# Splitting the second mixer's input and the first mixer's attention rows into high and low parts, and starting the last accumulators from transposes

## The chip, the cores and the metric

The kernel runs on one core of a Trainium2 chip. The metric is the device time of one execution in microseconds; several runs are taken and their median is compared. One further execution is recorded by the profiler, and all profile rows come from that one.

The engines that matter here: PE multiplies matrices, DVE (VectorE) and ACT (ScalarE) do the elementwise work, and SP issues the DMAs that bring weights from HBM into SBUF. Each engine runs its own queue in order and waits on the others where it needs their results.

## The reference

It is a two-layer decoder trunk in float32 for one sequence of 256 positions and 1024 channels:

```python
def mixer_ab(h, w_in, conv_w, ln_g, ln_b, w_out):      # layer 0
    u = h @ w_in
    u_val, u_gate, q, k, v = jnp.split(u, ...)
    ya = conformer_conv(u_val, u_gate, conv_w, ln_g, ln_b)
    yb = moba_attention(q, k, v)
    return jnp.concatenate([ya, yb], axis=-1) @ w_out

def mixer_c(h, w_in, conv_w, conv_b, w_r, b_r, w_i, b_i, lam, w_out):   # layer 1
    u = h @ w_in
    gate, xr = jnp.split(u, 2, axis=-1)
    xr = causal_depthwise_conv(xr, conv_w) + conv_b
    y = rg_lru(xr, w_r, b_r, w_i, b_i, lam) * jax.nn.gelu(gate)
    return y @ w_out

def sq_relu_mlp(h, w_up, w_down):
    return jnp.square(jax.nn.relu(h @ w_up)) @ w_down

def reference(x, ...):
    for layer in range(2):
        x = x + mixer(rmsnorm(x, mix_norm[layer]), ...)
        x = x + sq_relu_mlp(rmsnorm(x, mlp_norm[layer]), w_up[layer], w_down[layer])
    return rmsnorm(x, final_norm)
```

`rg_lru` applies block-diagonal gate matrices (8 blocks of 128 x 128 for r and for i) and a scan over the positions. `w_up` is 1024 x 4096, `w_down` 4096 x 1024. All weights, some 97 MB, are read once.

## The kernel before

**Layout.** The residual stream lives in SBUF transposed: eight tiles `xT[k]`, 128 channels by 256 positions. A product is 128 rows of a weight by 128 columns (the stationary operand) times a 128 x 256 activation tile, summed over k in a PSUM bank. There are four banks `bank_a` (accumulators of output projections) and four banks `bank_b` (everything else).

**Weights.** They come in pieces of 1 MB, two DMAs of 512 KB each; a piece has two units, and a unit is 128 x 1024 weights, eight products. A piece lands either in one of five `raw` buffers or in one of eight pairs `wh`/`wl`, used as plain storage. `piece` decides this with a counter: after five unsplit pieces in a row the next ones go to pairs.

**Two kinds of product.** An unsplit unit is multiplied in plain fp32: one instruction per product, which the profile shows as two records. A split unit lies in a raw buffer first; `weights` rounds it to `wh` (two moves of 128 x 512, on ACT or DVE, line 395 or 396) and subtracts to get `wl` (two DVE subtractions of 128 x 512). The activation is split likewise by `split_act`, and the product is three matmuls in fp32r: high by high, high weight by low activation, low weight by high activation. In the kernel before, only the MLP weights are split. Both mixers' weights are unsplit.

**Order of the work.** Nothing is issued when the Python code runs. The calls (`mms`, `tt`, `move`, `act`, `dma`, ...) add operations to a `Plan`, with an estimated cost on each engine; the plan then schedules all of them as a list, chooses ACT or DVE for each `move`, and emits them (line 310, so that almost every row of the profile names line 310). The order on each engine is therefore fixed before the run, and a change in one place can move instructions on every engine.

**Stages in the profile.** First mixer to about 125 us: projections, attention, a layer norm whose sums over channels are made by matmuls with `ones`, and the output projection over eight units `u_o` (4 to 7 are the attention rows, 0 to 3 the convolution rows). First MLP to about 308 us: 32 units of `w_up` and 32 of `w_down`, interleaved. Second mixer to about 398 us: eight units `u_xr` (recurrent branch: `xr_proj`, `xr_tail` with the convolution of width 4, `gates`, the scan) and eight units `u_gt` (`gate_chunk`), then the output projection `u_co`. Second MLP to the end. `residual_chunk` adds an output projection to `xT` and makes the next stage's activations; `finish_norm` makes 1/rms (`rstd`), which is multiplied in later, after the first products.

**The last residual.** In the second MLP the down projection is computed the other way round: the activation is the stationary operand, and five accumulators (`blocks`) hold positions by channels, so that the output needs no transposing. `xT` must be transposed into them to be added. `down_rows` does it at the steps 4 to 19: it splits `xT[k]` into high and low (tiles `r`), and multiplies each with an identity `identr`, 32 matmuls in all.

Of the kernel before, what the change touches and what calls it, by code (L numbers as in the profile page):

```python
# [7 lines left out]
F32R = mybir.dt.float32r  # L8
# [3 lines left out]
P = 128  # L12
S = 256
# [313 lines left out]
def hybrid_trunk(ctx, tc, x, mix_norm, mlp_norm, w_up, w_down, ab_w_in, ab_conv_w, ab_ln_g, ab_ln_b,  # L327
# [8 lines left out]
    def tl(name, shape=(P, S), dt=F32):  # L336
        return sb.tile(list(shape), dt, name=name)
# [48 lines left out]
    def copy(out, a):  # L386
        return plan.add("V", [("tensor_copy", (out, a), {})], [out], [a], {"V": vcost(fsize(out), not is_psum(a))})
# [37 lines left out]
    def transposes(items):  # L425
        calls = [("transpose", (o, i, d), {}) for o, i, d in items]
        return plan.add("T", calls, [items[0][0]], [i for _, i, _ in items] + [items[0][2]],
                        {"T": 0.109 * len(items)})

    def dma(out, in_, size):  # L430
        return plan.add("S", [("dma_start", (out, in_), {})], [out], [in_], {"S": 0.0}, size=size)


    ident = tl("ident", (P, P))
    identr = tl("identr", (P, P), F32R)
    ones = tl("ones", (P, P))
    pcol = tl("pcol", (P, P))
    wcol = tl("wcol", (P, P))
# [60 lines left out]

    pieces, units = [], []
    homes, pairs = [], {}
    turn = {"raw": 0, "pair": 0, "whole": 0}

    def piece(kind, ap, whole=True):
        n = len(pieces)
        pieces.append((kind, ap))
        us = [len(units), len(units) + 1]  # L510
        units.extend([(n, 0), (n, 1)])
        turn["whole"] = turn["whole"] + 1 if whole else 0
        if turn["whole"] > NRAW:
            i = turn["pair"] % NSPL
            turn["pair"] += 1
            homes.append((whs[i], wls[i]))
        else:
            raw = raws[turn["raw"] % NRAW]
            turn["raw"] += 1
            homes.append((raw[:, :1024], raw[:, 1024:]))  # L520
        if not whole:
            for u in us:
                pairs[u] = turn["pair"] % NSPL
                turn["pair"] += 1
        return us

    def cols(w, c, whole=True):

        return piece("c", w.rearrange("(k p) c -> p k c", p=P)[:, :, c * P:(c + 2) * P], whole)

    def rows(ap, whole=True):
        return piece("r", ap, whole)

    taken = [0, 0]
    got = {}
# [51 lines left out]
    for us in (((u_gate, 4), (u_val, 0)), ((u_q, 8), (u_k, 12))):  # L587
        for c in (0, 2):
            for u, at in us:
                u += cols(w_in, at + c)  # L590
    u_v = rows(wv[:, 0:4]) + rows(wv[:, 4:8])
    wo = ab_w_out[0].rearrange("(k p) c -> p k c", p=P)
    u_o = {}
    for k in (4, 6, 0, 2):
        u_o[k], u_o[k + 1] = rows(wo[:, k:k + 2])
    LAG, TAIL = 4, 4

    def mlp_units(layer):
        up, dn = [], []
        wd = w_down[layer].rearrange("(f p) c -> p f c", p=P)  # L600
        for f in range(0, NF + LAG, 2):
            if f < NF:
                up += cols(w_up[layer], f, False)
            if f >= LAG:
                dn += rows(wd[:, f - LAG:f - LAG + 2], False)
        return up, dn

    u_up, u_dn, u_xr, u_gt, u_co = {}, {}, [], [], []
    u_up[0], u_dn[0] = mlp_units(0)
    for c in range(0, 8, 2):  # L610
        u_xr += cols(c_w_in[0], 8 + c)
        if c == 2:
            u_r, u_i = piece("ri", None)
    for c in range(0, 8, 2):
        u_gt += cols(c_w_in[0], c)
    wco = c_w_out[0].rearrange("(k p) c -> p k c", p=P)
    for k in range(0, 8, 2):
        u_co += rows(wco[:, k:k + 2])
    u_up[1], u_dn[1] = mlp_units(1)


# [9 lines left out]
    xsrc = x[0].rearrange("(t p) d -> p t d", p=P)  # L631
    R = lambda ap: ap.rearrange("a (b p) -> (a b) p", p=P)
    make_identity(nc, ident)
    copy(identr, ident)
    memset(ones, 1.0, "V")
    memset(eps_t, EPS, "V")
    act(tiny[:, 60:61], eps_t, AF.Sqrt)
# [29 lines left out]
    def par(name, c):  # L667
        i = col0[name] + c
        return pcol[:, i:i + 1]


    def project(dst, u, xs):
        w = weights(u)
        for k in range(KD):
            mms([(dst, w[k], xs[k], k == 0, k == KD - 1)])

    def project_wide(b, u, xs):

# [19 lines left out]

    def residual_chunk(k, acc, gname, g0, xs):
        tt(xT[k], acc, xT[k], OP.add)  # L700
        g = par(gname, g0 + k)
        xs[k] = scaled(xT[k], g) if gname == "mix" else split_act(xT[k], g, "x", KD)
        if k in (0, KD - 2):
            act(ssum if k == 0 else sumb, xT[k], AF.Square)
        else:
            sq = rot("nsq", 2)
            act(sq, xT[k], AF.Square)
            if k < KD - 2:
                tt(ssum, ssum, sq, OP.add)
            else:  # L710
                tt(sumb, sumb, sq, OP.add)
# [136 lines left out]
    def pv(h):  # L848
        c, r = divmod(h, 2)
        if r == 0:  # L850
            oB[c] = bank("b")
        vs = slice(64 * h, 64 * h + 64)
        up, lo = (oB[c][:, u * P + 64 * r:u * P + 64 * r + 64] for u in range(2))
        mms([(up, pT[h][:, P:S], vt[:, 0, vs], r == 0, False), (up, pT[h][:, S:384], vt[:, 1, vs], False, True)])
        mms([(lo, pT[h][:, :P], vt[:, 0, vs], False, True)])
        if r == 0:
            return
        den, o = dens[c], arot("of", 2, S)
        recip(den, den)
        n = list(den.ap)  # L860
        wide = bass.AP(tensor=den.tensor, offset=den.offset, ap=[n[0], [1, 4], [0, 64]])
        tt(o.rearrange("p (a b) -> p a b", a=4), oB[c][:, :S].rearrange("p (a b) -> p a b", a=4), wide, OP.mult)
        b = bank("b")
        transposes([(b[:, u * P:(u + 1) * P], o[:, (1 - u) * P:(2 - u) * P], ident) for u in range(2)])
        mx[4 + c] = arot("mo", 4, S)
        move(mx[4 + c], b[:, :S])

    for c in range(2, 4):
        gate_unit(c)
# [61 lines left out]
        t = [bank("a") for _ in range(4)]  # L931
        return [t[c // 2][:, (c % 2) * S:(c % 2 + 1) * S] for c in range(KD)]

    def out_mm(acc, c, w, xp, start, stop):
        if not isinstance(w, tuple):
            return mms([(acc, w[c], xp, start, stop)])
        mms([(acc, a[:, c, :], b, start and n == 0, stop and n == 2)
             for n, (a, b) in enumerate(((w[0], xp[0]), (w[0], xp[1]), (w[1], xp[0])))])

    def out_rows(accs, u, xp, first):  # L940
        w = weights(u)
        for c in range(KD):
            out_mm(accs[c], c, w, xp, first and c % 2 == 0, False)

    def out_cols(accs, us, xps, done):
        ws = [weights(u) for u in us]
        for c0 in range(0, KD, 2):
            for c in (c0, c0 + 1):
                for i, (w, xp) in enumerate(zip(ws, xps)):
                    out_mm(accs[c], c, w, xp, False, i == len(us) - 1)  # L950
            done(c0)
            done(c0 + 1)

# [52 lines left out]
    out_cols(accs, us, hs, next_norm(accs, "mix", KD, xs))  # L1006


    for t in ("lg", "pT", "of", "mo"):
        pools.pop(t)  # L1010
    top[0] = 0
    spx = ar(3, KD)
# [128 lines left out]

    blocks = []

    def down_mm(block, w, hp, first, last):
        t, c0, c1, b = block
        s = slice(t * P, (t + 1) * P)
        wh, wl = (q.rearrange("p a b -> p (a b)")[:, c0:c1] for q in w)
        mms([(b[:, :c1 - c0], p[:, s], q, first and n == 0, last and n == 2)
             for n, (p, q) in enumerate(((hp[0], wh), (hp[1], wh), (hp[0], wl)))])

    xsp = {}

    def down_rows(u, hp, d):
        w = weights(u)
        if d == 0:
            blocks.extend((t, c0, c1, bank("a")) for t, c0, c1 in ((0, 0, 512), (0, 512, D), (1, 0, 512), (1, 512, 768)))
            blocks.append((1, 768, D, banks["b"].pop(bank_at["b"] % 4)))
        for block in blocks:
            down_mm(block, w, hp, d == 0, False)
        if 4 <= d < 20:  # L1160

            k, t = divmod(d - 4, 2)
            if t == 0:
                xsp[k] = split_act(xT[k], None, "r", 2)
            for bt, c0, c1, b in blocks:
                if bt == t and c0 <= k * P < c1:
                    mms([(b[:, k * P - c0:(k + 1) * P - c0], q[:, t * P:(t + 1) * P], identr, False, False)
                         for q in xsp[k][:2]])

    _, us, hs = mlp(1, xs, down_rows)  # L1170
    ws = [weights(u) for u in us]
# [2 lines left out]
    for n, block in enumerate(blocks):  # L1174
        t, c0, c1, b = block
        xg, fc = xg2[t], fcol[:, t]
        for i in range(len(us)):
            down_mm(block, ws[i], hs[i], False, i == len(us) - 1)

        part = fc[:, n % 2 if n < 2 else n - 2:][:, :1]  # L1180
        act(fsq[:, :c1 - c0], b[:, :c1 - c0], AF.Square, accum=part)
        tt(xg[:, c0:c1], b[:, :c1 - c0], gfin[:, c0:c1], OP.mult)
        if c1 < D:
            ts(fc[:, 4:5], part, 1.0 / D, EPS if c0 == 0 else fc[:, 4:5], OP.mult, OP.add)
            continue
        act(fc[:, 5:6], part, AF.Sqrt, scale=1.0 / D, bias=fc[:, 4:5])
        recip(fc[:, 6:7], fc[:, 5:6])
        for h in (slice(0, 512), slice(512, D)):
            move(xg[:, h], xg[:, h], fc[:, 6:7])
            dma(o_dst[:, t, h], xg[:, h], P * 2048)  # L1190
# [32 lines left out]
```

## Time and profile before

| | us |
|---|---|
| median of 3 runs | 589.08 (588.99 to 589.18) |
| the profiled execution | 588.62 |
| its span, first to last instruction | 586.8 |
| PE busy | 579.9 (99%) |
| DVE busy | 413.1 (70%) |
| ACT busy | 289.7 (49%) |

A group row reads: line, engine, operation, output <- inputs with shapes, count | busy time in all, mean ns of one | idle time of the engine just before, and which engine's work ended that idle time. A timeline row reads: start, length in us, engine, line, operation, count. Rows of the chain that ended last read: start, length, engine and tile, count. Buffer numbers are left out of names in the profile. Because instructions of one engine overlap at their ends, the distance from one start to the next is shorter than the duration.

### The profile page before, as it was taken

The numbers are of one execution on the slowest core, as the hardware profiler recorded it, in microseconds if no ns is written. First come the engines' busy times: TensorE is split into PE (matmuls) and PEld (weight loads), VectorE is DVE, ScalarE is ACT, GpSimd is POOL, SyncE is SP. The second block draws the span as 40 slices with busy tenths as digits, with TensorE's granted clock in tenths as the row PEclk, the third lists the DMA queues.
The fourth block names the chain that finished last, engine by engine and source line by source line (L and its number), as shares of the span: only waits on it lengthen the run. The fifth ranks groups of instructions, "written<-read, shape, count | busy, mean of one in ns | idle before, by whom it ended". The sixth has DMA issues, their size and how long they took to land.

```text
span 586.8 us, 9026 instructions
## 1 busy us (share of the span) xinstructions
PE 579.9 (99%) x3305; PEld 510.2 (87%) x3305; DVE 413.1 (70%) x946; ACT 289.7 (49%) x592; POOL 2.8 (0%) x22
## 2 busy tenths in 40 slices
PE   9999999999999999999999999999999999999995
PEld 8888768889999999999998888888888888888885
DVE  2599998599777767677446777559876767767732
ACT  4131435467554555555321798327555555545523
POOL 1000000000000000000000000000000000000000
PEclk9999999999999999999999999999999999999999
DMA  7997704125664665566677005924645664563001
GB/s 222 324 382 256 258 1 144 71 70 163 203 212 145 191 217 166 166 205 203 218 223 280 1 0 157 370 83 143 196 164 180 196 198 144 185 212 107 1 1 72
DMA packets 67612, 98.74 MB, mean 168 GB/s; under 512 B 3212, under 2 KB 55664, under 8 KB 67568
## 3 DMA queue, kind: packets, MB, share of 16 engines
q1 hardware_dynamic: 67568, 98.17, 50.7%
q8 instruction: 26, 0.43, 0.3%
q14 instruction: 18, 0.15, 0.1%
HBM read 97.11 MB, written 1.05 MB: 167 GB/s over the span
## 4 chain that ended last, share of the span: by engine, by line
PE 99%; ACT 0%; DVE 0%; issue 0%; ACTq 0%
PE bank_b L310 56%; PE bank_a L310 42%; ACT arena L395 0%; DVE arena L310 0%; ACT arena L310 0%; DVE ones L310 0%; DVE tiny L310 0%; DVE eps L310 0%; ACTq L310 0%
## 5 line engine op out<-in xcount | busy, mean ns | idle before, releaser
L310 DVE TENSOR_TENSOR wl<-raw,wh 128x512 fp32r<-128x512 f32 x256 | 175.1, 690 | 84.5 <-ACT wh L395 76.3
L395 ACT ACTIVATE wh<-raw 128x512 fp32r<-128x512 f32 x223 | 139.5, 630 | 168.2 <-PE bank_b L310 104.3
L310 PE MATMUL bank_b<-x,wh 128*128 128x512 f32 x512 | 184.7, 401 | 0.0
L310 PE MATMUL bank_b<-x,wl 128*128 128x256 f32 x512 | 143.8, 281 | 0.0
L310 PEld LDWEIGHTS bank_b<-x,wh 128*128 128x128 f32 x512 | 96.4, 188 | 20.9
L310 PEld LDWEIGHTS bank_b<-x,wl 128*128 128x128 f32 x512 | 96.8, 189 | 0.1
L310 PE MATMUL bank_a<-f,wh 128*128 128x256 f32 x512 | 93.2, 283 | 0.0
L310 PEld LDWEIGHTS bank_a<-f,wh 128*128 128x128 f32 x512 | 79.6, 191 | 1.4
L310 PE MATMUL bank_a<-f,wl 128*128 128x256 f32 x256 | 72.4, 283 | 0.0
L310 PE MATMUL bank_a<-wh,f 128*128 128x512 f32 (+1 forms) x256 | 72.2, 364 | 0.0
L310 PE MATMUL bank_b<-xg,raw 128*128 128x256 f32 x288 | 64.1, 379 | 0.0
L310 PEld LDWEIGHTS bank_b<-xg,raw 128*128 128x128 f32 x288 | 54.1, 190 | 7.3
L310 PEld LDWEIGHTS bank_a<-wh,f 128*128 128x128 f32 x256 | 45.9, 188 | 9.1
L310 DVE SCALAR_TENSOR_TENSOR arena<-arena,wcol 128x256 f32<-128x256 f32 x120 | 49.5, 478 | 0.0
L310 PEld LDWEIGHTS bank_a<-f,wl 128*128 128x128 f32 x256 | 49.0, 192 | 0.0
L310 PE MATMUL bank_a<-wl,f 128*128 128x512 f32 (+1 forms) x128 | 46.5, 363 | 0.0
L310 PE MATMUL bank_a<-arena,wh 128*128 128x256 f32 x128 | 34.4, 381 | 0.0
L310 PE MATMUL bank_a<-arena,wl 128*128 128x256 f32 x128 | 33.9, 379 | 0.0
L310 DVE TENSOR_TENSOR relu<-bank_b,relu 128x256 f32<-128x256 f32 x64 | 26.7, 417 | 10.1 <-ACT relu L310 10.1
L310 ACT ACT_TABLE_LOAD x24 | 30.8, 1283 | 3.0 <-PE bank_b L310 1.9
L310 ACT ACTIVATE relu<-relu 128x256 f32<-128x256 f32 x64 | 26.1, 411 | 8.2 <-DVE relu L310 5.1
L310 ACT ACTIVATE relu<-bank_b 128x256 f32<-128x256 f32 x64 | 23.6, 369 | 11.6 <-PE bank_b L310 11.6
(125 smaller groups left out, 594.3 us busy)
## 6 DMA issues: line engine op xcount, KB each, us to landing
raw<-in_w_up_dram SPq DMA_DIRECT2D x64, 512.0 KB, 5.7
raw<-in_w_down_dram SPq DMA_DIRECT2D x64, 512.0 KB, 4.8
raw<-in_c_w_in_dram SPq DMA_DIRECT2D x8, 512.0 KB, 5.4
raw<-in_ab_w_in_dram SPq DMA_DIRECT2D x6, 512.0 KB, 7.8
wh<-in_ab_w_in_dram SPq DMA_DIRECT2D x5, 512.0 KB, 8.7
wl<-in_ab_w_in_dram SPq DMA_DIRECT2D x5, 512.0 KB, 8.8
raw<-in_ab_w_in_dram SPq DMA_DIRECT2D x8, 256.0 KB, 5.7
wh<-in_ab_w_out_dram SPq DMA_DIRECT2D x4, 512.0 KB, 10.0
```

Of the source, the lines that this page charges most:

```text
L310: r.append(getattr(self.engines[o.eng], method)(*map(sub, a), **{n: sub(v) for n, v in k.items()}))
L395: return e.activation(sub(out), sub(a), AF.Copy, **({"scale": scale} if ap else {}))
```

## The change

It has four parts.

1. The input weights of the second mixer (`u_xr`, `u_gt`, 16 units) become split units, and their activations come from `split_act`. `project` uses a new function `mm`, which does one plain product for an unsplit unit and three fp32r matmuls for a split one.
2. The attention rows of the first output projection (`u_o[4]` to `u_o[7]`) become split units; the attention outputs `mx[4..7]` are split straight from the PSUM bank, in place of a move.
3. The place of each piece is named at its call ("raw", "pair" or "split") in place of the counter. With it, the r and i gate weights and `c_w_out` go to pairs.
4. The last residual: 16 transposes (fp32 through `ident`) of `xT` start the five accumulators at step 0. The splits of `xT`, the 32 matmuls with `identr`, and `identr` itself go.

```diff
+    def flip(out, in_, first):
+        return plan.add("T", [("matmul", (out,), {"lhsT": in_, "rhs": ident, "start": first, "stop": False, "is_transpose": True,
+                                                  "skip_group_check": True})], [out], [in_, ident], {"T": 0.109})
...
-    identr = tl("identr", (P, P), F32R)
...
-    def piece(kind, ap, whole=True):
+    def piece(kind, ap, place):
...
-        turn["whole"] = turn["whole"] + 1 if whole else 0
-        if turn["whole"] > NRAW:
+        if place == "pair":
             i = turn["pair"] % NSPL
...
-        if not whole:
+        if place == "split":
             for u in us:
                 pairs[u] = turn["pair"] % NSPL
...
-                u += cols(w_in, at + c)
-    u_v = rows(wv[:, 0:4]) + rows(wv[:, 4:8])
+                u += cols(w_in, at + c, "raw" if len(pieces) < NRAW else "pair")
+    u_v = rows(wv[:, 0:4], "pair") + rows(wv[:, 4:8], "pair")
...
-        u_o[k], u_o[k + 1] = rows(wo[:, k:k + 2])
+        u_o[k], u_o[k + 1] = rows(wo[:, k:k + 2], "split" if k > 3 else "pair")
...
-        u_xr += cols(c_w_in[0], 8 + c)
+        u_xr += cols(c_w_in[0], 8 + c, "split")
         if c == 2:
-            u_r, u_i = piece("ri", None)
+            u_r, u_i = piece("ri", None, "pair")
...
-        u_gt += cols(c_w_in[0], c)
+        u_gt += cols(c_w_in[0], c, "split")
...
-        u_co += rows(wco[:, k:k + 2])
+        u_co += rows(wco[:, k:k + 2], "pair")
...
+    def mm(dst, w, k, x, first, last):
+        ps = ((w[0][:, k], x[0]), (w[0][:, k], x[1]), (w[1][:, k], x[0])) if isinstance(w, tuple) else ((w[k], x),)
+        mms([(dst, a, b, first and n == 0, last and n == len(ps) - 1) for n, (a, b) in enumerate(ps)])
...
-            mms([(dst, w[k], xs[k], k == 0, k == KD - 1)])
+            mm(dst, w, k, xs[k], k == 0, k == KD - 1)
...
-        xs[k] = scaled(xT[k], g) if gname == "mix" else split_act(xT[k], g, "x", KD)
+        xs[k] = split_act(xT[k], par(gname, g0 + k), "x", KD)
...
-        mx[4 + c] = arot("mo", 4, S)
-        move(mx[4 + c], b[:, :S])
+        mx[4 + c] = split_act(b[:, :S], None, "x", KD)
...
         if d == 0:
...
+            for t, c0, c1, b in blocks:
+                for k in range(c0 // P, c1 // P):
+                    flip(b[:, k * P - c0:(k + 1) * P - c0], xT[k][:, t * P:(t + 1) * P], k * P == c0)
         for block in blocks:
-            down_mm(block, w, hp, d == 0, False)
-        if 4 <= d < 20:
-            k, t = divmod(d - 4, 2)
-            if t == 0:
-                xsp[k] = split_act(xT[k], None, "r", 2)
-            for bt, c0, c1, b in blocks:
-                if bt == t and c0 <= k * P < c1:
-                    mms([(b[:, k * P - c0:(k + 1) * P - c0], q[:, t * P:(t + 1) * P], identr, False, False)
-                         for q in xsp[k][:2]])
+            down_mm(block, w, hp)
```

**Where instructions moved.** Rows are in the order in which an engine runs them; a name's numbers are those of buffers and of their uses.

DVE in the second mixer, from the reciprocal of the norm on, before:

```order
L310 RECIPROCAL rstd<-rstd 128x256
L310 TENSOR_TENSOR arena<-bank_b_108,rstd 128x256
L310 TENSOR_TENSOR arena<-bank_b_109,rstd 128x256
L310 TENSOR_SCALAR arena<-arena,pcol 128x256 x2
L310 SCALAR_TENSOR_TENSOR arena<-arena,pcol 128x256 x6
L310 TENSOR_TENSOR arena<-bank_b_111,rstd 128x256
```

and now:

```order
L310 RECIPROCAL rstd<-rstd 128x256
L396 CAST wh_1_443<-raw_71 128x512
L310 TENSOR_TENSOR arena<-bank_b_107,rstd 128x256
L310 TENSOR_TENSOR arena<-bank_b_108,rstd 128x256
L310 TENSOR_SCALAR arena<-arena,pcol 128x256 x2
L310 SCALAR_TENSOR_TENSOR arena<-arena,pcol 128x256 x2
L310 TENSOR_TENSOR wl_1_700<-raw_71,wh_1_443 128x512
L310 SCALAR_TENSOR_TENSOR arena<-arena,pcol 128x256 x3
L310 TENSOR_TENSOR wl_1_700<-raw_71,wh_1_443 128x512
L310 SCALAR_TENSOR_TENSOR arena<-arena,pcol 128x256
L310 TENSOR_TENSOR arena<-bank_b_110,rstd 128x256
```

The convolution steps of `xr_tail` (the rows with `pcol`) now have the weights' subtractions (`wl`) among them.

PE at the second MLP's first down rows; before, one of the residual's pairs of products, and now the transposes, ahead of the first product into the accumulators:

```order
L310 MATMUL bank_b_111<-wl_3_3175,f_138 128x256
L310 MATMUL bank_a_104<-identr,r_144 128x128 x2
L310 MATMUL bank_b_108<-x_129,wh_3_3092 128x512
```

```order
L310 MATMUL bank_b_109<-x_129,wl_3_3480 128x256
L310 MATMUL bank_a_103<-ident,xT_91 128x128
L310 MATMUL bank_a_103<-ident,xT_92 128x128
L310 MATMUL bank_a_103<-ident,xT_93 128x128
L310 MATMUL bank_a_103<-ident,xT_94 128x128
```

Sixteen of these stand in one place, where before pairs like the one above were spread over sixteen steps.

SP's loads for the second mixer, before:

```order
L310 DMA raw_73<-in_c_w_in_dram 128x4x256 x2
L310 DMA raw_74<-in_c_w_in_dram 128x4x256 x2
L310 DMA raw_75<-in_c_w_r_dram 128x8x128
L310 DMA raw_75<-in_c_w_i_dram 128x8x128
L310 DMA raw_71<-in_c_w_in_dram 128x4x256 x2
L310 DMA raw_72<-in_c_w_in_dram 128x4x256 x2
L310 DMA wh_2_2499<-in_c_w_in_dram 128x4x256
L310 DMA wl_2_2505<-in_c_w_in_dram 128x4x256
```

and now:

```order
L310 DMA raw_74<-in_c_w_in_dram 128x4x256 x2
L310 DMA raw_70<-in_c_w_in_dram 128x4x256 x2
L310 DMA wh_2_2779<-in_c_w_r_dram 128x8x128
L310 DMA wl_2_2785<-in_c_w_i_dram 128x8x128
L310 DMA raw_71<-in_c_w_in_dram 128x4x256 x2
L310 DMA raw_72<-in_c_w_in_dram 128x4x256 x2
L310 DMA raw_73<-in_c_w_in_dram 128x4x256 x2
```

The gate weights r and i (`c_w_r`, `c_w_i`) went to a raw buffer and now go to a pair; the input pieces behind them went to two raw buffers and then to pairs, and now go to raw buffers only.

More of the change, by code (lines that the diff above doesn't have):

```diff
@@ L504, in hybrid_trunk @@
     homes, pairs = [], {}
-    turn = {"raw": 0, "pair": 0, "whole": 0}
-    def piece(kind, ap, whole=True):
+    turn = {"raw": 0, "pair": 0}
+    def piece(kind, ap, place):
         n = len(pieces)
@@ L525, in piece, with cols, rows @@
         return us
[L527 to L532, printed above, removed]
+    def cols(w, c, place):
+        return piece("c", w.rearrange("(k p) c -> p k c", p=P)[:, :, c * P:(c + 2) * P], place)
+    def rows(ap, place):
+        return piece("r", ap, place)
     taken = [0, 0]
@@ L602, in mlp_units @@
             if f < NF:
-                up += cols(w_up[layer], f, False)
+                up += cols(w_up[layer], f, "split")
             if f >= LAG:
-                dn += rows(wd[:, f - LAG:f - LAG + 2], False)
+                dn += rows(wd[:, f - LAG:f - LAG + 2], "split")
         return up, dn
@@ L633, in hybrid_trunk @@
     make_identity(nc, ident)
-    copy(identr, ident)
     memset(ones, 1.0, "V")
@@ L700, in residual_chunk @@
         tt(xT[k], acc, xT[k], OP.add)
-        g = par(gname, g0 + k)
-        xs[k] = scaled(xT[k], g) if gname == "mix" else split_act(xT[k], g, "x", KD)
+        xs[k] = split_act(xT[k], par(gname, g0 + k), "x", KD)
         if k in (0, KD - 2):
@@ L932, in accumulators @@
         return [t[c // 2][:, (c % 2) * S:(c % 2 + 1) * S] for c in range(KD)]
[L934 to L938, printed above, removed]
     def out_rows(accs, u, xp, first):
@@ L942, in out_rows @@
         for c in range(KD):
-            out_mm(accs[c], c, w, xp, first and c % 2 == 0, False)
+            mm(accs[c], w, c, xp, first and c % 2 == 0, False)
     def out_cols(accs, us, xps, done):
@@ L949, in out_cols @@
                 for i, (w, xp) in enumerate(zip(ws, xps)):
-                    out_mm(accs[c], c, w, xp, False, i == len(us) - 1)
+                    mm(accs[c], w, c, xp, False, i == len(us) - 1)
             done(c0)
@@ L1006, in hybrid_trunk @@
     out_cols(accs, us, hs, next_norm(accs, "mix", KD, xs))
-    for t in ("lg", "pT", "of", "mo"):
+    for t in ("lg", "pT", "of"):
         pools.pop(t)
@@ L1142, in hybrid_trunk, with down_mm @@
     blocks = []
-    def down_mm(block, w, hp, first, last):
+    def down_mm(block, w, hp, last=False):
         t, c0, c1, b = block
@@ L1147, in down_mm @@
         wh, wl = (q.rearrange("p a b -> p (a b)")[:, c0:c1] for q in w)
-        mms([(b[:, :c1 - c0], p[:, s], q, first and n == 0, last and n == 2)
+        mms([(b[:, :c1 - c0], p[:, s], q, False, last and n == 2)
              for n, (p, q) in enumerate(((hp[0], wh), (hp[1], wh), (hp[0], wl)))])
-    xsp = {}
     def down_rows(u, hp, d):
@@ L1177, in hybrid_trunk @@
         for i in range(len(us)):
-            down_mm(block, ws[i], hs[i], False, i == len(us) - 1)
+            down_mm(block, ws[i], hs[i], i == len(us) - 1)
         part = fc[:, n % 2 if n < 2 else n - 2:][:, :1]
```

## The prediction

> **What bounds the kernel now.** I read three views first: the page's busy times, its chain that ended last, and the waits of the PE queue.
>
> ```profile
> PE 579.9 (99%) x3305; PEld 510.2 (87%) x3305; DVE 413.1 (70%) x946; ACT 289.7 (49%) x592; POOL 2.8 (0%) x22
> PE 99%; ACT 0%; DVE 0%; issue 0%; ACTq 0%
> PE bank_a L310 <- DVE eps L310: 1.0, 1, 1.0
> ```
>
> The reader should see that TensorE is the whole path: 99% of the span, and one wait of 1.0 us, before the first matmul. So every matmul that goes, or gets shorter, shortens the program, as long as nothing else becomes late. What could become late is read stage by stage, since the 70% of DVE is a mean. In the windows below the columns are the length, then busy time of PE, PEld, DVE, ACT and POOL, clock, DMA share, GB/s.
>
> ```profile
> 15.00:68.50 53.50, 53.50 (x252) 46.00 (x251) 46.12 (x129) 12.42 (x25) 0.00 (x0) 1.00 0.97 331
> 68.50:105.00 36.50, 36.50 (x168) 25.36 (x168) 31.56 (x106) 16.02 (x45) 0.21 (x2) 1.00 0.19 64
> 105.00:125.00 20.00, 20.00 (x96) 17.58 (x95) 13.30 (x32) 9.79 (x21) 0.00 (x0) 1.00 0.14 53
> 290.00:308.00 18.00, 18.00 (x143) 17.57 (x142) 7.29 (x19) 4.59 (x12) 0.00 (x0) 1.00 0.71 225
> 308.00:339.00 31.00, 31.00 (x146) 27.26 (x145) 21.62 (x53) 15.50 (x28) 0.00 (x0) 1.00 0.34 133
> 339.00:370.00 31.00, 31.00 (x145) 27.28 (x144) 21.87 (x53) 27.16 (x44) 0.00 (x0) 1.00 0.36 111
> 370.00:398.00 28.00, 28.00 (x132) 24.43 (x131) 15.45 (x39) 8.23 (x18) 0.00 (x0) 1.00 0.56 197
> 398.00:412.00 14.00, 14.00 (x82) 12.28 (x81) 13.82 (x31) 11.12 (x24) 0.00 (x0) 1.00 0.51 153
> ```
>
> The first three rows are the first mixer (projections, attention, output projection). Rows four to seven are the end of the first MLP's output and the second mixer, where DVE is busy 66.2 of 108 us and ACT 55.5. The last row is the start of the second MLP: there DVE is busy 13.82 of 14.00 us and PE still never waits, so a full DVE queue is no wait as long as it is ahead.
>
> **The change part by part. What PE saves.** The price of a product is the distance from one start to the next, which is shorter than the duration printed in a group row.
>
> ```profile
> 346.76 1.89 PE L310 MATMUL bank_b<-xg,wl 128*128 128x256 f32 x8
> 348.48 1.03 PE L310 MATMUL bank_b<-arena,raw 128*128 128x256 f32 x4
> 139.16 2.87 PE bank_a L310 x24
> ```
>
> Eight plain records take 1.72 us (346.76 to 348.48): .215 each. A plain fp32 product is two records, .431. The third row, from the chain of waits, is 24 matmuls of split operands, 256 wide, in 2.87 us: .1197 each, three to a product, .359. A product that changes kind saves .072.
>
> The second mixer's input has 16 units of 8 products: 128 x .072 = 9.2 us. The four attention units of the first output projection have 32 products: 2.3 us.
>
> The last residual has these rows:
>
> ```profile
> 507.21 0.34 PE L310 MATMUL bank_a<-identr,r 128*128 128x128 f32 x2
> 507.38 0.45 PE L310 MATMUL bank_b<-x,wh 128*128 128x512 f32 x1
> 7.59 0.60 PE L310 MATMUL bank_a<-ident,arena 128*128 128x128 f32 x4
> 8.03 1.89 PE L310 MATMUL bank_b<-xg,raw 128*128 128x256 f32 x8
> 9.85 0.66 PE L310 MATMUL bank_a<-ident,arena 128*128 128x128 f32 x4
> 10.34 1.89 PE L310 MATMUL bank_b<-xg,raw 128*128 128x256 f32 x8
> ```
>
> Two products with `identr` take .17, so the 32 that go cost 2.7. Four transposes through `ident` take .44 or .49, so the 16 that come cost 1.8 to 2.0. That saves .8 to .9; I take .9. The eight splits of xT that fed them leave ACT or DVE in the second MLP, where PE did not wait for either, so they are worth nothing. The transposes need only xT, which has been final since before that MLP began, so they wait for nothing new. PE saves 9.2 + 2.3 + .9 = 12.4 us.
>
> **What it adds elsewhere.** Each split unit costs two moves (ACT or DVE) and two subtractions (DVE):
>
> ```profile
> L310 DVE TENSOR_TENSOR wl<-raw,wh 128x512 fp32r<-128x512 f32 x256 | 175.1, 690 | 84.5 <-ACT wh L395 76.3
> L395 ACT ACTIVATE wh<-raw 128x512 fp32r<-128x512 f32 x223 | 139.5, 630 | 168.2 <-PE bank_b L310 104.3
> 402.33 2.49 DVE L310 TENSOR_TENSOR wl<-raw,wh 128x512 fp32r<-128x512 f32 x4
> 405.21 0.43 DVE L396 CAST wh<-raw 128x512 fp32r<-128x512 f32 x1
> ```
>
> A subtraction lasts .690, but four in a row take 2.49, so the next can start after .60. For the second mixer that is 32 moves (20 us of ACT at .630) and 32 subtractions (19.2 us of DVE at .60), and eight low halves of the activations. DVE rises from 66.2 to about 88.6 us, in a stage that shrinks from 108 to 98.8: 90%, from 61%. For the first mixer it is 8 moves, 8 subtractions (4.8) and four low halves of the attention outputs (1.4).
>
> **Second mixer, the tight place.** There I counted instructions in the order of the changed program, from the reciprocal of the mixer's norm to the subtractions of the fourth gate unit, the last before DVE's queue thins out. Prices:
>
> ```profile
> 314.65 1.75 DVE L310 RECIPROCAL rstd<-rstd 128x256 f32<-128x256 f32 x1 [4.49 <-ACT rstd L310]
> 316.51 0.76 DVE L310 TENSOR_TENSOR arena<-bank_b,rstd 128x256 f32<-128x256 f32 x2
> 317.19 0.73 DVE L310 TENSOR_SCALAR arena<-arena,pcol 128x256 f32<-128x256 f32 x2
> 317.83 2.46 DVE L310 SCALAR_TENSOR_TENSOR arena<-arena,pcol 128x256 f32<-128x256 f32 x6
> 323.20 1.53 DVE L310 SCALAR_TENSOR_TENSOR arena<-arena,pcol 128x256 f32<-128x256 f32 x3
> 313.95 3.40 PE L310 MATMUL bank_b<-xg,raw 128*128 128x256 f32 x15
> ```
>
> From start to start: `rstd` products .34, `TENSOR_SCALAR` .32 to .41, a convolution step .40 among others and .52 in a dependent chain (the last two DVE rows). DVE: reciprocal 1.7, 23 subtractions 13.9, 24 convolution steps at .42 10.1, 10 `rstd` products 3.4, 8 `TENSOR_SCALAR` at .36 2.9, 2 moves .7, 5 further products 1.7: 34.4. The reciprocal starts .70 after the matmul of the sums has made room on PE (314.65 against 313.95), so DVE is done at 35.1. PE in the same stretch: 236 split matmuls at .1197 are 28.2, and 16 plain gate products at .431 6.9: 35.1 too. So the queue is exactly full, and what DVE loses in it, waiting for a move on ACT or for a bank, PE waits for. Before, DVE was busy 21.62 of 31.00 us there (308 to 339).
>
> How much it loses no row shows directly. The least is the full queue at 398 to 412: .18 of 14, which makes .4 here. The most is a queue that meets each move late, as in the MLPs: 84.5 us over 256 subtractions is .33 each, and 23 of them make 7.6. I take 2.3: nearer the full queue, since ACT is not the slower one here (about 32 us of work in 35), but it carries seven table loads of 1.28 us, which stand in its queue ahead of moves.
>
> **First mixer.** PE reaches the layer norm's sums 2.4 us sooner, or less.
>
> ```profile
> 101.06 0.42 DVE L310 TENSOR_TENSOR sumb<-sumb,nsq 128x256 f32<-128x256 f32 x1
> 103.42 0.59 PE L310 MATMUL bank_b<-sumb,ones 128*128 128x256 f32 x2
> L310 ACT ACT_TABLE_LOAD x24 | 30.8, 1283 | 3.0 <-PE bank_b L310 1.9
> ```
>
> DVE has the second sum at 101.48; PE takes it at 103.42. That is 1.9 us of slack. The order moves some twenty operations on 8 columns behind this point, which pays on DVE for the new subtractions ahead of it. So PE's gain of 2.4 leaves a wait of about .5. Behind it, DVE and ACT were busy half to two thirds of 105 to 125, and the rest fits. I take .7; the bounds are 0 (the queue ahead shortens as much) and 3 (all 6.2 us of new DVE work lie ahead of the sums, less the slack and the small operations).
>
> **The loads.** All second-mixer input pieces now pass through the five raw buffers. The gate weights r and i go to a pair that is free only when the first MLP's last products are done, and the pieces behind them in SP's queue wait with them.
>
> ```profile
> raw<-in_c_w_in_dram SPq DMA_DIRECT2D x8, 512.0 KB, 5.4
> ```
>
> From issue to landing is 5.4 us, queueing included. 512 KB at the 331 GB/s of the first window is 1.6 us, so the 2 MB of r, i and the next piece take 6.4 us from that moment. PE has four units of 2.87 us (11.5) already split to work on. I cost the loads at nothing; without that cover the first late piece would cost up to 3.
>
> **The sum.** The profiled execution took 588.62 us. 588.62 - 12.4 + .7 + 2.3 = 579.2. The median of the runs, 589.08, is .46 above it, so I predict 579.7.
>
> **The rivals.**
>
> A. All the added work hides: DVE runs as at 398 to 412, and the sums come early as well. 589.08 - 12.4 = 576.7. For it: a queue at 99% without a PE wait stands in the profile. Against: that queue had been ahead; this one starts at the reciprocal, level with PE.
>
> C. DVE meets each move late, as in the MLPs: 7.6 instead of 2.3, 585.0. For it: 90% of DVE over the whole stage, and the table loads ahead of moves. Against: these waits in the MLPs occur with nothing else in the queue to do.
>
> D. Slower: the splits are not ahead of PE at all in the second mixer. Each of the 12 units behind the r and i weights lands late and goes through move (.630) and subtraction (.690) with PE waiting: 12 x 1.32 = 15.8, giving 593.2. It decides once a unit costs over (12.4 - .7) / 12 = .98 us on average. For it: the queue order on SP, and raw buffers which now come free only after a split. Against: PE needs 5.7 us for a piece that takes 3.2 us to move.
>
> E. One wait is long enough for the clock to fall back. At the start, PE ran slowly for a time:
>
> ```profile
> 1.05 3.36 PE bank_a L310 x14
> ```
>
> 14 plain matmuls 128 wide took .24 each, against .215 / 2 = .108 for that width later: half speed for 3.4 us. If one wait brings this back, it costs 1.7 on top; with a wait of 3.4 in place of 2.3 that is 582.5. No wait in this trace is long enough to show it. The Trainium skill's page "TensorE: Matmul & The Clock Gate", Part 1 on the HAM clock gate, says the clock halves after about 3.4 us idle and returns after as long a busy stretch; the slow start here agrees with the second half of that.
>
> F. The products do not get shorter, because PE meets the operands of the split units late by as much: no change.
>
> **Chances.** A .25, the forecast .40 (577.5 to 582 by itself), C .18, E .06, D .07, F .04. The likeliest is the forecast, 579.7. The range 576.3 to 585.8 holds A, the forecast, E and C. A measurement of this kernel tells .2% from no change: faster .89 (A, forecast, C, E), same .04 (F), slower .07 (D).
>
> **What would show it.** Right: PE's instructions fall into the same places, with a split product at .36 in the second mixer; 16 transposes at .11 ahead of the second MLP's first down rows; waits of PE on DVE `wl` of some 2 us, mostly between the reciprocal and the fourth gate unit; DVE close to full there; under 1 us at the layer norm. Wrong: PE waits for a `raw` load or for ACT's moves; a wait at the start of the second MLP (DVE still behind); transposes at more than .2 each; or a granted clock below 1 after a wait.

## The result and the profile after

The changed kernel takes 575.85 us (median, 575.59 to 576.09), against 589.05 before: a ratio of 0.9775, 95% interval 0.9759 to 0.9792, or 13.2 us less. The forecast was 579.7, with a range from 576.3, so the time lies half a microsecond below the range. The direction was right, and so was the main mechanism (PE bounds the kernel, and its saving reaches the end); the gain was larger than forecast by 3.9 us. The profiled execution took 576.05 us, its span 574.3.

The page of the changed kernel (its busy times and the shares of the chain that ended last), and the waits of its PE queue:

```profile
PE 565.7 (99%) x3449; PEld 504.5 (88%) x3449; DVE 435.7 (76%) x991; ACT 304.7 (53%) x620; POOL 2.7 (0%) x22
PE 84%; DMA 7%; ACT 4%; SPq 4%; issue 1%; DVE 0%; ACTq 0%
PE bank_a L310 <- DVE eps L310: 1.0, 1, 1.0
PE bank_a L310 <- DMA arena<-in_x_dram: 0.9, 1, 0.9
PE bank_b L310 <- DVE arena L310: 0.5, 1, 0.5
PE bank_b L310 <- DVE wl L310: 0.2, 1, 0.2
```

PE is still busy 99% of the span. DVE has 22.6 us more to do and ACT 15.0, and in the second mixer PE waits for all that work .2 us in one place. The chain no longer lies on PE alone, because it is followed back through the waits of .2 and .5 us to ACT and to loads; the shares are those of the work in front of two short waits, not time that PE lost.

The other two new waits lie in the first 46 us. The one of .9, for the input `x`, is of a kind that runs without the change show too (.3 in the kernel before with wider identity products, below). The one of .5 belongs to the change:

```profile
43.96 1.15 ACT L395 ACTIVATE wh<-raw 128x512 fp32r<-128x512 f32 x2 [8.89 <-DMA raw<-in_ab_w_out_dram]
44.62 0.69 DVE L310 TENSOR_TENSOR wl<-raw,wh 128x512 fp32r<-128x512 f32 x1 [1.14 <-ACT wh L395]
```

The first attention unit's weights land at about 44 us; ACT rounds them, DVE stands 1.14 us at their subtraction, and behind it in DVE's queue is the product that PE needs at 45.79. Of the nine profiled executions with split attention rows six show this wait (.17 to 1.08 us), of the five without none does.

The stretch that the prediction counted as exactly full, in windows of the changed kernel; then the end of that stretch on DVE and on PE, from the timeline:

```profile
310.40:345.20 34.80, 34.70 (x264) 33.51 (x262) 33.62 (x74) 29.18 (x51) 0.00 (x0) 1.00 0.71 233
```

```profile
310.40 1.75 DVE L310 RECIPROCAL rstd<-rstd 128x256 f32<-128x256 f32 x1 [1.81 <-ACT rstd L310]
...
342.78 0.68 DVE L310 TENSOR_TENSOR wl<-raw,wh 128x512 fp32r<-128x512 f32 x1
344.51 0.69 DVE L310 TENSOR_TENSOR wl<-raw,wh 128x512 fp32r<-128x512 f32 x1 [1.04 <-ACT wh L395]
```

```profile
345.26 0.39 PE L310 MATMUL bank_b<-x,wl 128*128 128x256 f32 x1 [0.15 <-DVE wl L310]
```

From the reciprocal on, DVE has no idle time for 33 us; then it waits once, 1.04 us, for a move on ACT, and the subtraction that follows is the one PE waits for. The place is the one the prediction named, the fourth gate unit. DVE lost 1.04 us there, and the .15 at the end is what reached PE. ACT has no idle time between the following row and that move; its own wait there ended when a `raw` piece had landed, so followed back the wait begins at a load:

```profile
322.25 0.63 ACT L395 ACTIVATE wh<-raw 128x512 fp32r<-128x512 f32 x1 [1.38 <-DMA raw<-in_c_w_in_dram]
```

Where the 12.5 us between the two spans come from is read from the chain that ended last, at places that both kernels have, first before and then now (68.61 and 69.85 are the first 512-wide products of the first mixer):

```profile
68.61 13.93 PE bank_a L310 x32
142.03 2.83 PE bank_b L310 x16
412.22 2.42 PE bank_a L310 x12
579.48 1.45 PE bank_b L310 x12
```

```profile
69.85 1.91 PE bank_a L310 x4
140.22 2.83 PE bank_b L310 x16
401.68 1.53 PE bank_a L310 x14
403.20 0.22 PE bank_b L310 x2
403.42 2.44 PE bank_a L310 x12
566.86 1.45 PE bank_b L310 x12
```

| stage | forecast | measured |
|---|---|---|
| first mixer to its 512-wide products (68.61 against 69.85) | 0 | +1.2 |
| first mixer behind them (142.03 against 140.22, less the 1.2) | -1.6 | -3.05 |
| second mixer (412.22 against 401.68, less the 1.8 so far) | -6.9 | -8.7 |
| transposes (401.68 to 403.42) and steps without the old residual | -.9 | -2.1 |
| after the last matmul row | 0 | +.1 |
| sum | -9.4 | -12.5 |

The +1.2 holds the waits of .9 and .5, less .5 because the first products start sooner (5.83 against 6.30 us); it differs from run to run. The -3.05 does not: all nine profiled executions with split attention rows have it within .1 us. The transposes take 1.74 us, 16 at .109, as priced.

### The profile page after: what moved, and what is told of

Same layout as the page of the kernel before. It is cut to its first block, busy times and chain, and to the rows that moved or that the text cites. A ratio compares the mean times of both kernels' runs of the same rounds, so it can differ in the third digit from the quotient of the medians.

```text
span 574.3 us, 9432 instructions
## 1 busy us (share of the span) xinstructions
PE 565.7 (99%) x3449; PEld 504.5 (88%) x3449; DVE 435.7 (76%) x991; ACT 304.7 (53%) x620; POOL 2.7 (0%) x22
## 3 DMA queue, kind: packets, MB, share of 16 engines
HBM read 97.11 MB, written 1.05 MB: 171 GB/s over the span
## 4 chain that ended last, share of the span: by engine, by line
PE 84%; DMA 7%; ACT 4%; SPq 4%; issue 1%; DVE 0%; ACTq 0%
PE bank_b L310 43%; PE bank_a L310 41%; SPq L310 4%; DMA raw<-in_c_w_in_dram 3%; DMA raw<-in_ab_w_out_dram 2%; ACT arena L310 1%; ACT wh L395 1%; ACT L310 1%; DMA arena<-in_ab_conv_w_dram 1%; DMA raw<-in_ab_w_in_dram 1%; DVE arena L310 0%; DVE wl L310 0%; ACT arena L395 0%; DVE tiny L310 0%; ACTq L395 0%
## 5 line engine op out<-in xcount | busy, mean ns | idle before, releaser
L310 DVE TENSOR_TENSOR wl<-raw,wh 128x512 fp32r<-128x512 f32 x296 | 201.8, 689 | 81.4 <-ACT wh L395 79.6
L310 PE MATMUL bank_b<-x,wh 128*128 128x512 f32 (+1 forms) x768 | 231.3, 362 | 0.0
L310 PE MATMUL bank_b<-x,wl 128*128 128x256 f32 x640 | 180.3, 282 | 0.2 <-DVE wl L310 0.2
L310 PEld LDWEIGHTS bank_b<-x,wh 128*128 128x128 f32 x768 | 136.8, 190 | 21.2 <-ACT arena L310 0.2
L310 PEld LDWEIGHTS bank_b<-x,wl 128*128 128x128 f32 x640 | 121.6, 190 | 0.5 <-DVE wl L310 0.4
L310 PE MATMUL bank_b<-xg,raw 128*128 128x256 f32 x160 | 35.8, 380 | 0.0
L310 PEld LDWEIGHTS bank_b<-xg,raw 128*128 128x128 f32 x160 | 29.9, 190 | 4.0 <-DVE arena L310 0.2
L310 DVE TENSOR_TENSOR f<-relu,f 128x256 fp32r<-128x256 f32 x64 | 26.7, 419 | 2.2 <-ACT f L395 2.2
L310 DVE SCALAR_TENSOR_TENSOR relu<-relu,rstd 128x256 f32<-128x256 f32 x64 | 26.8, 424 | 1.8
L310 PEld LDWEIGHTS bank_a<-wl,f 128*128 128x128 f32 x128 | 24.1, 188 | 3.9
```

The lines of the kernel that those rows point to most:

```text
L310: r.append(getattr(self.engines[o.eng], method)(*map(sub, a), **{n: sub(v) for n, v in k.items()}))
```

## The experiments

**One part alone, one part undone.** The changed kernel itself ran beside the last group of experiments only. Elsewhere its 575.85 stands for it; the kernel before, which ran beside every group, moved between 588.76 and 589.05.

The first kernel splits only the second mixer's input.

```diff
-        u_o[k], u_o[k + 1] = rows(wo[:, k:k + 2], "split" if k > 3 else "pair")
+        u_o[k], u_o[k + 1] = rows(wo[:, k:k + 2], "pair")
...
-        mx[4 + c] = split_act(b[:, :S], None, "x", KD)
+        mx[4 + c] = arot("mo", 4, S)
+        move(mx[4 + c], b[:, :S])
...
-            for t, c0, c1, b in blocks:
-                for k in range(c0 // P, c1 // P):
-                    flip(...)
+        if 4 <= d < 20:
+            (split of xT[k] and products with identr, as before)
```

> The kernel with the second mixer's input split (and the new places of the pieces) and nothing else of the change. Theory P (all of the split products' gain reaches the end, the full DVE queue of the second mixer holds): 128 products x .072 = 9.2, so about 579.9 against 589.1, PE waits under 0.5 us. Rival R (the gain of the whole change came mostly from elsewhere, the second mixer gives what was forecast, 9.2 less 2.3): about 582.2 with 2 us of PE waits on wl.

Measured: 580.19 us (579.34 to 581.76) against 588.99, 8.8 us less, and its two fastest runs 9.6 less. The size is theory P's. In the profiled execution, the slowest of the four, PE waits in the tight stretch all the same, 1.2 us for a bank that ACT has to empty and .2 for `wl`: more than P's .5, and not R's 2 us on `wl`. Ahead of it DVE had waited for a load:

```profile
316.07 0.43 DVE L396 CAST wh<-raw 128x512 fp32r<-128x512 f32 x1 [1.55 <-DMA raw<-in_c_w_in_dram]
341.81 0.50 PE L310 MATMUL bank_b<-x,wh 128*128 128x256 f32 x2 [1.19 <-ACT arena L310]
```

In this execution the second mixer gained 7.3 us and not 8.7.

The second undoes the same attention rows in the changed kernel and keeps the rest.

> The changed kernel with the attention rows of the first output projection unsplit again. Theory P: it loses 32 products x .072 = 2.3 us, 578.1 against 575.9. Rival R (the first mixer's own order and its waits decide, the split rows bring little): within 0.8 us of the changed kernel.

Measured: 578.56 us (578.46 to 579.02), 2.7 us slower than the changed kernel's 575.85. Theory P, somewhat over its 2.3, and what is over is not scatter: from the 512-wide products to the first MLP's first row of 24 products this kernel takes 70.6 us, as do the kernel before and the two other kernels here whose attention rows are unsplit, and the changed kernel 67.5.

The third makes only the last residual's change, in the kernel before.

```diff
-            down_mm(block, w, hp, d == 0, False)
-        if 4 <= d < 20:
-            (split of xT[k] and products with identr)
+            down_mm(block, w, hp, False, False)
...
+            for t, c0, c1, b in blocks:
+                for k in range(c0 // P, c1 // P):
+                    flip(b[:, k * P - c0:(k + 1) * P - c0], xT[k][:, t * P:(t + 1) * P], k * P == c0)
```

> The kernel before with the last residual by 16 transposes and nothing else. Theory T (a 128-wide split matmul beside 512-wide ones hides less of the weight load behind it than its start-to-start time shows, so that the 32 identity products cost 3.9 us and not 2.7): 2.1 us faster than before, 587.0. Rival U (32 x .085 = 2.7 less 1.8): 0.9 faster, 588.2.

Measured: 586.57 us against 588.99, ratio 0.9961 (0.9946 to 0.9976), 2.4 us less. This is theory T's size. The three parts alone make 8.8 + 2.7 + 2.4 = 13.9, near the 13.2 of all together.

**What a short matmul costs.** Two steps of the second MLP's middle, from the chain of the kernel before, and the same two steps of the changed kernel:

```profile
437.37 0.17 PE bank_a L310 x2
437.55 2.87 PE bank_b L310 x16
440.42 2.45 PE bank_a L310 x12
442.87 0.36 PE bank_b L310 x3
443.22 0.17 PE bank_a L310 x2
...
449.04 0.17 PE bank_a L310 x2
```

```profile
537.70 2.40 PE bank_a L310 x12
540.10 3.19 PE bank_b L310 x19
543.29 2.40 PE bank_a L310 x12
```

A step with a pair of identity products is 5.85 or 5.82 us long (437.37 to 443.22 to 449.04), a step without is 5.59. The pair costs .245, though its own row shows .17. The rest is in the rows behind it: 2.87 + .36 where 3.19 stands without, and 2.45 for 2.40. To see what makes it so, the transposes were first taken apart, one to a step:

```diff
-            for t, c0, c1, b in blocks:
-                for k in range(c0 // P, c1 // P):
-                    flip(b[:, k * P - c0:(k + 1) * P - c0], xT[k][:, t * P:(t + 1) * P], k * P == c0)
-        for block in blocks:
-            down_mm(block, w, hp)
+        for block in blocks:
+            down_mm(block, w, hp, False, d == 0)
+        if 4 <= d < 20:
+            k, t = divmod(d - 4, 2)
+            for bt, c0, c1, b in blocks:
+                if bt == t and c0 <= k * P < c1:
+                    flip(b[:, k * P - c0:(k + 1) * P - c0], xT[k][:, t * P:(t + 1) * P], False)
```

> The changed kernel with the 16 transposes one at each of the steps 4 to 19 in place of all before step 0. Theory T (a short matmul standing alone leaves part of the next weight load uncovered): each transpose costs .16 to .20 in place of .11, 0.8 to 1.4 us slower than the changed kernel, and the step's length shows it. Rival U (a transpose costs .11 wherever it stands): the same time within 0.2.

Measured: 575.44 us (574.80 to 577.88), within the scatter of the changed kernel, and the steps are 5.66 and 5.72 us: .07 to .13 for a transpose. So theory T in that form is false: standing alone costs a transpose nothing extra. It was mended: a split matmul takes .12 however few columns it has, because the next weight load takes that long, and a pair hands part of its bill to the rows behind it. If so, a pair of 256 columns must cost the same as a pair of 128.

```diff
-    identr = tl("identr", (P, P), F32R)
+    identr = tl("identr", (P, 3 * P), F32R)
...
+    ts(identr[:, :P], ident, 0.0, None, OP.mult)
+    ts(identr[:, 2 * P:], ident, 0.0, None, OP.mult)
...
-                    mms([(b[:, k * P - c0:(k + 1) * P - c0], q[:, t * P:(t + 1) * P], identr, False, False)
+                    j = k // 2 * 2
+                    mms([(b[:, j * P - c0:(j + 2) * P - c0], q[:, t * P:(t + 1) * P], identr[:, (j + 1 - k) * P:(j + 3 - k) * P], False, False)
                          for q in xsp[k][:2]])
```

> The kernel before, with each of the 32 products of the last residual made 256 columns wide in place of 128: the identity has a block of zeros beside it, which adds nothing to the neighbouring columns. Theory T, mended (a split matmul costs .12 however short, since the next weight load takes that long; a 128-wide one only shows part of it in its own start-to-start time): a pair stays at .24 to .25, the same time as before within 0.3 us. Rival U (128-wide costs .085, 256-wide .12): 32 x .035 = 1.1 us slower than before.

Measured: 588.71 us against 588.90, ratio 0.9996 (0.9987 to 1.0006). Twice the columns cost nothing. The chain of that kernel:

```profile
437.75 0.24 PE bank_a L310 x2
437.99 2.82 PE bank_b L310 x16
440.81 2.45 PE bank_a L310 x12
443.26 0.36 PE bank_b L310 x3
443.62 0.23 PE bank_a L310 x2
```

The pair's own row now shows .24 and the rows behind it are shorter (2.82 and 2.77 for 2.87); the step, 5.87 and 5.78, is as long as with 128 columns. That a split matmul of 128 columns costs as much as one of 256 is shown, in this place. That the weight load sets the .12 fits the rows but was not measured apart.

**Is the DVE queue of the second mixer really full?** In the changed kernel the first DVE operation of each convolution branch was done twice, with the order of everything else kept.

```diff
-        tt(xp[:, 3:], b[:, :S], rstd, OP.mult)
+        plan.add("V", [("tensor_tensor", (xp[:, 3:], b[:, :S], rstd), {"op": OP.mult})] * 2, [xp[:, 3:]], [b[:, :S], rstd],
+                 {"V": vcost(S)})
```

> The changed kernel with the first DVE operation of each of the eight convolution branches in the second mixer done twice (same result, same order of everything else): 8 x .34 = 2.7 us more on DVE in the stretch that was counted as exactly full. Theory F (the queue is full: DVE idled 1.0 us there, .2 of it reached PE): DVE ends 2.7 - 1.0 later, so PE waits about 1.7 to 1.9 us there and the kernel is 1.5 to 1.7 us slower. Rival S (there is slack that the count does not see): slower by under 0.3.

Measured: 578.13 us, 2.3 us slower than the changed kernel. The waits in its PE timeline:

```profile
338.59 0.70 PE L310 MATMUL bank_b<-arena,wh 128*128 128x256 f32 x2 [1.38 <-DVE arena L310]
347.59 0.39 PE L310 MATMUL bank_b<-x,wl 128*128 128x256 f32 x1 [1.03 <-DVE wl L310]
```

The two ends of the stretch on DVE:

```profile
310.19 1.75 DVE L310 RECIPROCAL rstd<-rstd 128x256 f32<-128x256 f32 x1 [1.81 <-ACT rstd L310]
...
346.25 1.28 DVE L310 TENSOR_TENSOR wl<-raw,wh 128x512 fp32r<-128x512 f32 x2
```

PE waits 2.4 us in that stretch in place of .15, and DVE waits for nothing in it any more: its 1.04 us of idle time is gone. From the reciprocal to the start of the last subtraction (.60 after 346.25) it takes 36.7 us, against 34.1 with 1.04 of idle time. So the eight operations cost 3.6 us, .45 each and not the .34 of the expectation, and the 2.6 by which DVE ends later comes out on PE as 2.3. Theory F holds, and its 1.7 to 1.9 was small by the price of a repeated operation. The count was right to within a microsecond, and the queue has no slack.

**How far it can be taken.** The same split for the second mixer's output, where DVE still idled 7.0 of 42.0 us in the changed kernel:

```profile
345.00:387.00 42.00, 41.84 (x247) 38.32 (x247) 35.00 (x86) 28.67 (x55) 0.00 (x0) 1.00 0.77 264
```

First the last four of the eight units, then all of them, then all of them with POOL allowed for the subtractions. The edit of the first:

```diff
-    u_co += rows(wco[:, k:k + 2], "pair")
+    u_co += rows(wco[:, k:k + 2], "split" if k > 3 else "pair")
...
-        mx[c] = gi[c]
+        mx[c] = split_act(gi[c], None, "x", KD) if c > 3 else gi[c]
```

> The changed kernel with the last four of the eight output units of the second mixer split too, with their four activations. PE saves 32 x .072 = 2.3 us. DVE gets 8 subtractions (4.8) and 4 low halves (1.4), 6.2 us, between the gate units and the second MLP, where it idles about 7 us now. Theory F (a full queue costs nothing until it is behind): 2 us faster than the changed kernel. Rival C (DVE meets the start of the second MLP late): gain under 0.7 us, with PE waits on wl or x at the start of the second MLP.

> All eight output units of the second mixer split. PE saves 64 x .072 = 4.6 us; DVE gets 12.3 us where it idles about 7, in a stretch that gets 4.6 shorter. Theory F: DVE is late by up to 9.7 less what can be done earlier or later, so the gain is eaten: between 1 us faster and 3 us slower than the changed kernel, with waits of PE on wl. Rival S: 4.6 us faster.

> As the kernel with all eight output units split, but their subtractions and the low halves of their activations may go to POOL, which idles; nine or ten of them do. The price of such a subtraction on POOL is in no trace so far. If it is under 2.5 us each and DVE is not slowed beside it, the kernel is 3 to 4.6 us faster than the changed kernel; if POOL takes much longer, PE waits for it and the gain is gone.

Measured: 573.78, 574.54 and 582.34 us. In these three kernels the split activations share buffers with activations that are still read, so some products use overwritten values; the amount of work is what the text says. Four units gain 2.1 us, as theory F said. All eight gain only 1.3 of 4.6: in the profiled execution PE waits 1.5 us for ACT and 1.05 in three pieces for DVE (`x`) between 344 and 387, and DVE is busy 41.2 of the 42.0 us; the remaining .7 was not traced. On POOL it is a loss of 6.5 us, which the last section takes up.

Then four units again, two of whose four activations have buffers of their own, so that nothing is overwritten while it is still read; beside it the changed kernel, and the same with the transposes spread:

> The changed kernel once more, beside the next two: 575.9 within 0.5.

> The last four output units of the second mixer split, as in the earlier run, but two of the four split activations have buffers of their own, so that nothing is overwritten while it is still read (in the earlier run the next norm's activations overwrote them, so its output was another). Theory F: PE saves 2.3, DVE stays in time: 573.8, 2 us faster than the changed kernel. Rival C: the other order that the new buffers give brings waits of 1 us and more on DVE in the second mixer: 575.

> As the one before, with the transposes one at each of the steps 4 to 19: the same time within 0.3, since a transpose cost .10 alone and .11 in a row.

Measured: 576.03 (575.10 to 577.06), 574.46 (573.52 to 575.23) and 574.29 us (573.81 to 574.87). Both medians are below the changed kernel's, by 1.6 and 1.7 of the 2 us expected, though the range of the first just touches its range; against before the ratios are 0.9754 (0.9739 to 0.9768) and 0.9752 (0.9737 to 0.9767). Windows of the first of them:

```profile
345.00:387.00 42.00, 42.00 (x293) 39.88 (x292) 40.87 (x98) 34.83 (x70) 0.00 (x0) 1.00 0.73 250
```

DVE is now busy 40.87 of these 42.0 us, and PE waits for nothing in them.

## Why the prediction was wrong, point by point

**What bounds the kernel, and the gain of a split product: right.** The saving reached the end: the second mixer gained 8.7 of the 9.2.

**"How much it loses no row shows directly ... I take 2.3": this step failed.** The DVE work was counted as 34.4 and PE's as 35.1; measured, DVE was busy 33.6 in 34.8 us and PE waited .15. What failed was the allowance on top. Its upper end came from the MLPs' waits, .33 per subtraction, and the value was put between the ends because of the table loads on ACT. But a wait in a queue that has nothing else to do does not carry over to a queue with work standing in it: here DVE lost 1.04 us in one piece, and the doubled operations made even that vanish. The lower end, .4 from the full queue at 398 to 412, was the row of the same kind and should have been taken; with it the sum is 1.9 lower. It was a near thing all the same: 3.6 us more work on DVE cost 2.3, and a later load brought 1.4 us of waits in the first experiment.

**First mixer, "2.3 us" less "I take .7": mis-sized, it saved 3.05.** There PE waited for nothing at the layer norm. The changed kernel's rows:

```profile
100.83 0.42 DVE L310 TENSOR_TENSOR sumb<-sumb,nsq 128x256 f32<-128x256 f32 x1
101.51 0.59 PE L310 MATMUL bank_b<-sumb,ones 128*128 128x256 f32 x2
```

DVE has the sum at 101.25 and PE takes it at 101.51: .26 of the former 1.9 us is left. PE came 1.9 us sooner, which is 3.1 that it had gained since the 512-wide products less the 1.2 that it had lost ahead of them; DVE came .2 sooner. So the .7 was not paid, and .75 was saved that the sum does not have. By start-to-start times, the products of the output projection became 1.9 us shorter (27.85 to 25.97) and the 99 records of short matmuls between them 1.2 shorter (14.40 to 13.20). Why the short ones did was not examined. Against this stands the wait at 45.79, .5 here, for which the prediction had no term.

**"So the 32 that go cost 2.7": mis-sized.** They cost 3.9, .12 each. The price was read from inside the pair; the length of a whole step, with and without one, would have given it. The 16 transposes cost 1.74, as said. So this part saves 2.1 and not .9.

**The loads at nothing: nearly right here, and partly luck.** No wait of PE on a weight load appears in the second mixer, though these loads now take 7.2 us from issue to landing, 5.4 before. But ACT waited for them there 5.5 us in seven pieces, and the first move on DVE could start at 312.18 us, .03 after DVE had done the reciprocal. Where that piece came later, the stage was longer: in the first experiment DVE waited 1.55 us for it, and PE then 1.4 in all; in the second, whose second mixer is the changed kernel's, DVE waited 1.94, PE .5, and the second mixer took .8 us longer than here. That the piece alone made these differences was argued from the order of the waits and not tested.

**The rivals.** A, everything hides, is the nearest, with 576.7 against 575.85. C's waits came as .15 us here and D's serial chain not at all. E needs a long wait: the longest seen is in the POOL run (last section).

**What carried the time out of the range.** For the profiled execution the forecast was 579.2, and 576.05 was measured. Of these 3.1 us the second mixer makes 1.8, the first mixer 1.45 and the residual 1.2, against 1.2 lost ahead of the 512-wide products and .1 at the end. The medians are 3.9 apart, because the forecast put the median .5 above the profiled execution and it lies .2 below. Too large an allowance alone would have left the time in the range: without any, the sum is A's 576.7. It fell out because PE's own saving was not the 12.4 of the sum but 14.3 (1.2 more from the residual, .75 from the first mixer), and no rival had a saving above 12.4.

## What to carry to other kernels

Price an instruction that stands between others by the length of a whole period with and without it, not by the distance to its neighbour. For a second engine whose queue is filled to the level of the first, count the work by start-to-start times and take the losses from a stretch where that queue is full, not from one where it idles; then the count alone says how much more can be moved there. When work trades one engine's time for another's, stop where the other engine's busy time in that stage reaches its length: here four units of the next projection still paid 1.6 to 2.1 us, and eight paid less, 1.3. And ask of each new load in a full stage when it lands: here PE waited .15 us in the stage, and .5 and 1.4 us in two executions in which one piece landed 1.5 to 1.9 us later.

## What the runs showed of the hardware that was not expected

**POOL slows DVE.** With all eight output units split and POOL taking ten of the weights' subtractions (and one low half), POOL and DVE rows of the same moment:

```profile
353.18 4.39 POOL L310 TENSOR_TENSOR wl<-raw,wh 128x512 fp32r<-128x512 f32 x3 [1.96 <-DMA raw<-in_c_w_out_dram]
```

```profile
353.50 2.95 DVE L310 TENSOR_TENSOR arena<-arena 128x256 f32<-128x256 f32 x2
356.37 1.75 DVE L310 TENSOR_TENSOR wl<-raw,wh 128x512 fp32r<-128x512 f32 x1
```

```profile
L310 DVE TENSOR_TENSOR arena<-arena 128x256 f32<-128x256 f32 x25 | 15.0, 622 | 0.1
L310 DVE TENSOR_TENSOR arena<-bank_b,rstd 128x256 f32<-128x256 f32 x7 | 2.9, 411 | 0.0
```

Two DVE products that take .76 together elsewhere took 2.95, about as long as two of POOL's subtractions beside them (1.5 each). In the groups of 340 to 395 us the products with both inputs in SBUF rise to .622 on average (.419 with all on DVE), those with one input in PSUM stay at .411, also the two of them that ran inside a POOL subtraction (350.00 and 362.71 us). A move from SBUF to SBUF beside POOL took 1.51 us (at 363.48) where .43 is usual. The Trainium skill's page "SBUF — State Buffer", section "SBUF: two separate sides", says that DVE instructions with two SBUF inputs and POOL instructions hold a shared pair of ports exclusively, each for a whole instruction; the rows of the products with two SBUF inputs agree.

**The clock after a wait of 3.2 us.** In the same run PE waited once 3.16 us, and the window behind it:

```profile
359.09 0.39 PE L310 MATMUL bank_b<-x,wh 128*128 128x256 f32 x1 [3.16 <-DVE x L310]
359.10:362.00 2.90, 2.90 (x24) 2.90 (x25) 2.90 (x9) 2.05 (x5) 0.08 (x1) 1.00 0.08 17
```

24 matmuls in 2.90 us, .12 each, at a granted clock of 1.00: a wait of this length did not bring the clock back to half. Rival E's mechanism stays untested beyond that.

**The floor of a split matmul.** .12 us with 128 columns as with 256. The Trainium skill's page "TensorE: Matmul & The Clock Gate", Part 2, "Back-to-back issue gap", gives about 81 ns for a stream of 128-column matmuls with their weight loads. By that the 32 products would have cost 2.6, an estimate; the .085 inside a pair looked like it, and the steps measured .12.
